# Strassen's seven products of each pair of gemms, spread farther apart, in a macaron decoder layer

## The chip, the cores and the metric

The kernel runs on one core of a Trainium2 chip. The metric is the device time of one execution in microseconds. The kernel before was timed in three runs: 2215.63 us in the median, from 2208.47 to 2218.6.

## What is computed

One decoder layer on 256 tokens of width 2048, in float32: a SwiGLU half, a mixer (attention with dilated windows beside a gated MLP), a second SwiGLU half, and a norm. The change concerns the two SwiGLU halves:

```python
D_MODEL = 2048
SEQ = 256
D_FF = 5632
...
def swiglu(x, w_gate, w_up, w_down):
    return (jax.nn.silu(x @ w_gate) * (x @ w_up)) @ w_down
...
  x = x + 1/2 * SwiGLU_1(rms(x))
  x = x + mixer
  x = x + 1/2 * SwiGLU_2(rms(x))
```

## The kernel before

**Products.** Every float32 operand is split into a high and a low part, and a product is three matmuls: high by high, high by low, low by high. The activations (256 tokens, two tiles of 128) are stationary, and a weight tile of 128 rows and 512 columns streams through. Weights are split on the way: ScalarE copies the rounded high part into `wh` (line 227), VectorE subtracts it and leaves the low part in `wl` (line 228). There are four pairs of `wh` and `wl` (`LA + 1`).

**Steps.** The weights of a gemm (512 columns) come in units of four row tiles, 1 MB in one DMA on SP's queue, into three rotating buffers `raw`. A unit makes two ordinary steps ("n" in the list `steps`) of two row tiles; one is 12 matmuls (2 row tiles, 2 token tiles, 3 products). The main loop emits the products of step i and then the splits of the step four ahead (`advance`), so that in each engine's queue the splits run four steps ahead of the matmuls. All engines work strictly through their queues in the order in which this loop writes them, so the list `steps` sets the order of everything. `at(i, fn)` puts other work (SiLU, the turning of a result through DRAM, norms) at a place in this order.

**Quads.** Two gemms on the same activations (gate and up of the same 512 columns, or two column blocks of down) share one chunk of four row tiles in which Strassen's scheme (Winograd's form) is used. The 2 x 2 blocks are: the two token tiles and the two halves of the row tiles on the side of the activations, and the two halves of the row tiles (first index) and the two gemms (second index) on the side of the weights: b11, b21, b12, b22, each of two tiles of 512 columns, 512 KB. Instead of eight block products there are seven, p1 to p7. Each is a quad step ("s") of 6 matmuls. There are 27 quads: 19 in gate/up pairs, 8 in down pairs. A gate/up pair is a cycle of 12 ordinary steps and 7 quad steps, 186 matmuls.

The order of a quad is p1, p6, p7, p5 (the list OPEN, put between the last four ordinary steps of the pair before) and p2, p4, p3 (CLOSE, put between the first four of its own), so that one ordinary step lies between two of them. Each of p1, p6, p7 and p5 adds into the same PSUM bank `x_`, and after each a copy or sum of that bank goes elsewhere before the next may add to it: after p1 ScalarE copies it into q11 (line 285), after p6 into `part` (line 289), after p7 into q21 (line 291) with a subtraction on VectorE (line 293), and after p5 VectorE adds `part` into q12 (line 295).

The weights' side of p5, p6, p7 and p4 are sums of blocks. VectorE makes three of them in a row ahead of p6's split, and one ahead of p4's (`form_of`, lines 204 to 209). The first two overwrite b11 and b12.

The blocks of a quad lie in one tile `quad`. Its room is asked for anew (`room_for`) when the last quad step, p3, of the quad before has been split; then four pieces of 512 KB follow, two behind each of the next two units.

Of the kernel before, what the change touches and what calls it, by code (L numbers as in the profile page):

```python
# [44 lines left out]
def layer(ctx: ExitStack, tc: tile.TileContext, a, out):  # L45
# [54 lines left out]
    gemms = []  # L100
    hus = []
    steps = []
    ends = []
    callbacks = []
    counter = itertools.count()
# [3 lines left out]
                          quad=quad, steps=0, begun=[False] * NT, left=[3 * nk] * NT))  # L109


    OPEN = ("p1", "p6", "p7", "p5")
    CLOSE = ("p2", "p4", "p3")

    def lay_out():
        i = 0
        while i < len(gemms):
            g = gemms[i]
            size, stage = g["group"]
            chunk = g["quad"] and g["quad"]["chunk"]  # L120
            order = [(p, q) for p in range(size) for q in range(gemms[i + p]["nk"] // 2)
                     if not g["quad"] or q // 2 != chunk]
            if stage:
                order.sort(key=lambda s: stage(*s, gemms[i + s[0]]["nk"] // 2))
            new = [("n", (gemms[i + p], q // 2, q % 2)) for p, q in order]
            if g["quad"]:
                quad = g["quad"]
                quad["gemms"] = gemms[i], gemms[i + 1]
                tail = steps[-4:]
                del steps[-4:]  # L130
                for old, form in zip(tail, OPEN):
                    steps.extend((old, ("s", (quad, form))))
                for k, form in enumerate(CLOSE):
                    new.insert(2 * k + 1, ("s", (quad, form)))
                for h in quad["gemms"]:
                    h["left"] = [3 * (h["nk"] - 4) + 6] * NT
                gemms[i + 1]["left"][1] += 18
            steps.extend(new)
            i += size
        t = -1.0  # L140
        for kind, s in steps:
            t += 1 if kind == "n" else 0.5
            ends.append(t)
            if kind == "n":
# [35 lines left out]
            SP.dma_start(raws[i][:, first:end], src[:, first + o:end + o])  # L180
            first = end

    pieces = []
    quads = []

    def room_for(quad):
        quad["raw"] = big.tile([P, 8, NC], F32, tag="C", name=f"quad{len(quads)}")
        quads.append(quad)
        pieces.extend((quad, b) for b in (0, 2, 1, 3))

    def load_piece():
        quad, b = pieces.pop(0)
        g = quad["gemms"][b // 2]
        k0 = g["rows0"] + (4 * quad["chunk"] + 2 * (b % 2)) * P
        src = g["w"][k0:k0 + 2 * P, g["c0"]:g["c0"] + NC].rearrange("(k p) c -> p k c", p=P)
        SP.dma_start(quad["raw"][:, 2 * b:2 * b + 2], src)

    def block(quad, g, j):
        return quad["raw"].rearrange("p (g q j) c -> p g j q c", g=2, q=2)[:, g, j]

    def form_of(quad, form):
        b11, b21, b12, b22 = (block(quad, g, j) for g in range(2) for j in range(2))
        if form == "p6":
            DVE.tensor_tensor(b11, b12, b11, op=OP.subtract)  # L204
            DVE.tensor_tensor(b12, b12, b22, op=OP.subtract)  # L205
            quad["sum"] = big.tile([P, 2, NC], F32, tag="k2", name="sum")
            DVE.tensor_tensor(quad["sum"], b22, b11, op=OP.subtract)  # L207
        elif form == "p4":
            DVE.tensor_tensor(b21, b21, quad["sum"], op=OP.subtract)  # L209
        return {"p1": b11, "p2": b21, "p3": b22, "p4": b21, "p5": b11, "p6": quad["sum"] if form == "p6" else None,  # L210
                "p7": b12}[form]

    place = {}

    def split(i, k=slice(0, 2)):
        kind, s = steps[i]
        if kind == "n":
            m = place[i]
            r = raws[m // 2][:, 2 * (m % 2):2 * (m % 2) + 2, :]
        else:  # L220
            r = form_of(*s)
        if i not in splits:
            wh = big.tile([P, 2, NC], F32R, tag="wh", bufs=LA + 1, name=f"wh{i}")
# [3 lines left out]
        ACT.activation(wh[:, k], r[:, k], AF.Copy)  # L227
        DVE.tensor_tensor(wl[:, k], r[:, k], wh[:, k].bitcast(F32), op=OP.subtract)  # L228
# [38 lines left out]
    def quad_products(i, quad, form):  # L267
# [7 lines left out]
        for q in range(2):  # L275
# [5 lines left out]
            for act, w in ((hi, wh), (hi, wl), (lo, wh)):  # L281
                product(g, t, act, w[:, q], q == 1 and act is lo)
        (q11, q21), (q12, x_) = first["ps"], second["ps"]
        if form == "p1":
            ACT.activation(q11, x_, AF.Copy)  # L285
            first["begun"][0] = True
        elif form == "p6":
            quad["part"] = sb.tile([P, NC], F32, tag="W", name="part")
            ACT.activation(quad["part"], x_, AF.Copy)
        elif form == "p7":  # L290
            ACT.activation(q21, x_, AF.Copy)
            first["begun"][1] = True
            DVE.tensor_tensor(quad["part"], quad["part"], x_, op=OP.subtract)
        elif form == "p5":
            DVE.tensor_tensor(q12, x_, quad["part"], op=OP.add)  # L295
            second["begun"][0] = True
        close(g, i)

# [137 lines left out]
    def ffn(wg, wu, wd, down_post, group):  # L436
        sides[0] = 0
        halves = ((0, 6), (6, 11))
        for hf, (f0, f1) in enumerate(halves):
# [8 lines left out]
            for f in range(f0, f1):  # L448
# [38 lines left out]
                quad = dict(chunk=CS, forms=lambda: xT["forms"])  # L487
                gemm(wg, f * NC, 0, KD, lhs_x, post_gate, BOTH, bank, quad)
                gemm(wu, f * NC, 0, KD, lhs_x, post_up, BOTH, bank, quad)
            for c in range(4):  # L490
                if c % 2 == 0:
                    bank = side()
                    quad = dict(chunk=0, forms=lambda st=st: st["forms"])
# [3 lines left out]
        for g in gemms:  # L497
            g.setdefault("stage", wd)

    def side():  # L500
        sides[0] += 1
# [442 lines left out]
        sgw_turn(mixer + 8 + 10 * h, h)  # L944
    at(ends[-1] - 36, load_fin)
    for after, stage in ((12, a["ffn1_w_gate"][0]), (start_of(ffn2_gate) + 1, ffn2_gate)):
        at(after, lambda: room_for(next(q for i, (k, q) in enumerate(steps) if k == "s" and not q[0].get("raw"))[0]))


    load_unit(0, (0, 1))  # L950
# [149 lines left out]
```

## Time and profile before

| | |
|---|---|
| median of three runs | 2215.63 us |
| the profiled execution | 2210.57 us |
| its span, first to last instruction | 2208.9 us |
| mean granted clock of TensorE | 0.973 |
| mean rate of the DMA engines | 213 GB/s |
| instructions | 24108 |

The profile names engines PE (matmul), PEld (weight load), DVE (VectorE), ACT (ScalarE), POOL and SP; SPq is SP's DMA queue. Tiles are named out<-in, and L227 is line 227 of the kernel. `mm` and `qd` are PSUM banks (`qd` those of quads), `raw` the units, `quad` the blocks of a quad, `sum` the sum for p6, `fpx` and `fph` the sums of activations, `hlo`, `xlo` and so on the low parts of activations. A wait is named by who waits, then who ended it.

### The profile page before, as it was taken

The page shows a single profiled execution, that of the slowest core. Times are in us where ns is not written, and L with a number is a line of the kernel's source. Part 1 is how long each engine was busy: PE and PEld are TensorE (multiplying, and loading weights), DVE is VectorE, ACT ScalarE, POOL GpSimd, SP SyncE. Part 2 cuts the span into 40 slices and gives each one's busy share as a digit, 9 for nine tenths or more (in the row PEclk, how much of TensorE's full clock was granted, in tenths as well). Part 3 has the DMA queues.
Part 4 walks back from the last instruction along what each step waited for, and adds up shares of the span by engine and source line. Part 5 has one row for each costly group of instructions (what it writes and reads, how often), then busy time and mean ns, then how long its engine had stood idle before and what let it go on. Part 6 is the DMA issues. An engine that isn't in the chain of part 4 may idle for free.

```text
span 2208.9 us, 24108 instructions
## 1 busy us (share of the span) xinstructions
PE 2063.2 (93%) x9323; PEld 1771.9 (80%) x9323; DVE 1433.9 (65%) x1463; ACT 1088.6 (49%) x1240; POOL 11.3 (1%) x19
## 2 busy tenths in 40 slices
PE   9988999998889899999999999998998899978898
PEld 8777778876678788888888888877777788867787
DVE  6666667666667567666655555666665676666675
ACT  6544455444445555454554444554444454445454
POOL 0000000000000000000000000000000000000000
PEclk9999999999999999999999999999999999999999
DMA  8655666565556876697766666865566665655563
GB/s 308 206 184 203 210 221 220 187 206 188 173 190 210 255 259 210 212 281 257 261 214 225 225 216 226 260 199 189 182 214 198 216 219 188 215 186 175 190 229 134
DMA packets 249499, 471.54 MB, mean 213 GB/s; under 512 B 12460, under 2 KB 41000, under 8 KB 249256
## 3 DMA queue, kind: packets, MB, share of 16 engines
q1 hardware_dynamic: 249064, 469.47, 63.7%
q8 instruction: 73, 1.20, 0.2%
q10 hardware_dynamic: 320, 0.53, 0.1%
q14 instruction: 42, 0.34, 0.0%
HBM read 440.30 MB, written 29.66 MB: 213 GB/s over the span
## 4 chain that ended last, share of the span: by engine, by line
PE 55%; DMA 16%; DVE 14%; ACT 7%; issue 6%; SPq 1%; ACTq 0%; DVEq 0%; POOLq 0%; POOL 0%
PE mm L237 30%; PE qd L237 24%; DMA quad<-in_ffn_w_gate_dram 5%; ACT wh L227 5%; DVE wl L228 5%; DMA raw<-in_ffn_w_up_dram 3%; DMA quad<-in_ffn_w_down_dram 3%; DVE quad L205 1%; DMA xt<-bmx 1%; DVE quad L204 1%; DVE sum L207 1%; DVE quad L209 1%; DMA raw<-in_ffn_w_down_dram 1%; DMA uroom<-bmu 1%; DVE qd L295 1%
## 5 line engine op out<-in xcount | busy, mean ns | idle before, releaser
L228 DVE TENSOR_TENSOR wl<-raw,wh 128x1024 fp32r<-128x1024 f32 (+1 forms) x665 | 800.3, 1216 | 476.0 <-ACT wh L227 474.8
L227 ACT ACTIVATE wh<-raw 128x1024 fp32r<-128x1024 f32 (+1 forms) x665 | 695.0, 1050 | 628.1 <-PE mm L237 291.2
L237 PE MATMUL qd<-wl,xhi 128*128 128x512 f32 x1026 | 400.3, 390 | 14.8 <-DVE wl L228 14.6
L237 PE MATMUL qd<-wh,xhi 128*128 128x512 f32 x1026 | 399.6, 389 | 7.5 <-ACT wh L227 7.5
L237 PE MATMUL qd<-wh,xlo 128*128 128x512 f32 x1026 | 395.9, 386 | 0.0
L237 PE MATMUL mm<-wh,xhi 128*128 128x512 f32 x928 | 352.6, 380 | 2.0 <-ACT wh L227 2.0
L237 PE MATMUL mm<-wl,xhi 128*128 128x512 f32 x928 | 350.5, 380 | 4.1 <-DVE wl L228 3.9
L237 PE MATMUL mm<-wh,xlo 128*128 128x512 f32 x928 | 351.8, 379 | 0.0
L228 DVE TENSOR_TENSOR wl<-quad,wh 128x1024 fp32r<-128x1024 f32 x162 | 197.4, 1218 | 201.4 <-ACT wh L227 112.8
L227 ACT ACTIVATE wh<-quad 128x1024 fp32r<-128x1024 f32 x162 | 169.6, 1047 | 240.5 <-DMA quad<-in_ffn_w_gate_dram 87.6
L237 PEld LDWEIGHTS qd<-wl,xhi 128*128 128x128 f32 x1026 | 199.7, 195 | 57.9 <-DVE wl L228 26.9
L237 PEld LDWEIGHTS qd<-wh,xhi 128*128 128x128 f32 x1026 | 200.4, 195 | 40.5 <-ACT wh L227 10.3
L237 PEld LDWEIGHTS qd<-wh,xlo 128*128 128x128 f32 x1026 | 198.8, 194 | 28.5
L237 PEld LDWEIGHTS mm<-wl,xhi 128*128 128x128 f32 x928 | 175.4, 189 | 31.3 <-DVE wl L228 6.7
L237 PEld LDWEIGHTS mm<-wh,xhi 128*128 128x128 f32 x928 | 175.4, 189 | 27.5 <-ACT wh L227 2.8
L237 PEld LDWEIGHTS mm<-wh,xlo 128*128 128x128 f32 x928 | 175.4, 189 | 24.9 <-DVE xlo L398 0.3
L237 PE MATMUL qd<-wh,fpx 128*128 128x512 f32 x304 | 116.8, 427 | 74.8 <-ACT qd L285 74.1
L237 PEld LDWEIGHTS qd<-wh,fpx 128*128 128x128 f32 x304 | 63.6, 209 | 91.9 <-ACT qd L285 80.9
L227 ACT ACTIVATE wh<-sum 128x1024 fp32r<-128x1024 f32 x27 | 28.5, 1056 | 136.2 <-DVE sum L207 136.2
L237 PE MATMUL qd<-wh,hhi23.0_659 128*128 128x512 f32 x172 | 65.3, 380 | 0.9 <-ACT wh L227 0.9
L237 PE MATMUL qd<-wl,hhi23.0_659 128*128 128x512 f32 x172 | 65.3, 380 | 0.8 <-DVE wl L228 0.8
L237 PE MATMUL qd<-wl,hhi522.0_10636 128*128 128x512 f32 x172 | 65.3, 380 | 0.4 <-DVE wl L228 0.4
(400 smaller groups left out, 2289.3 us busy)
## 6 DMA issues: line engine op xcount, KB each, us to landing
raw<-in_w_in_dram SPq DMA_DIRECT2D x92, 1024.0 KB, 5.4
raw<-in_ffn_w_down_dram SPq DMA_DIRECT2D x72, 1024.0 KB, 5.3
raw<-in_ffn_w_gate_dram SPq DMA_DIRECT2D x66, 1024.0 KB, 5.2
raw<-in_ffn_w_up_dram SPq DMA_DIRECT2D x66, 1024.0 KB, 5.2
quad<-in_ffn_w_gate_dram SPq DMA_DIRECT2D x38, 512.0 KB, 7.8
quad<-in_ffn_w_up_dram SPq DMA_DIRECT2D x38, 512.0 KB, 8.7
quad<-in_ffn_w_down_dram SPq DMA_DIRECT2D x32, 512.0 KB, 8.5
raw<-in_w_out_dram SPq DMA_DIRECT2D x16, 1024.0 KB, 5.1
```

Source lines behind the costliest of these rows:

```text
L204: DVE.tensor_tensor(b11, b12, b11, op=OP.subtract)
L205: DVE.tensor_tensor(b12, b12, b22, op=OP.subtract)
L207: DVE.tensor_tensor(quad["sum"], b22, b11, op=OP.subtract)
L209: DVE.tensor_tensor(b21, b21, quad["sum"], op=OP.subtract)
L227: ACT.activation(wh[:, k], r[:, k], AF.Copy)
L228: DVE.tensor_tensor(wl[:, k], r[:, k], wh[:, k].bitcast(F32), op=OP.subtract)
L237: PE.matmul(g["ps"][t], act, in_turn(w), start=not g["begun"][t], stop=g["left"][t] == 0, skip_group_check=g["quad"] is not None)
L295: DVE.tensor_tensor(q12, x_, quad["part"], op=OP.add)
```

## The change

It does five things.

- The quad steps lie farther apart: p1, two ordinary steps, p6, two, p7, two (with the border of the pairs between), p5, two, p3, one, p2, one, p4.
- The four sums on VectorE are no longer made at p6 and p4. Each stands ahead of the split of another step (`prepared`): t1 = b12 - b11 two steps ahead of p1, t3 = b12 - b22 one step ahead of p1, t2 = b22 - t1 on the step behind p1, and t4 = b21 - t2 on the step ahead of p5. t1 and t2 have places of their own, so that b11 is no longer overwritten; t4 overwrites t2.
- There is one room for the blocks of all quads of an FFN. A block of the next quad is loaded into the place of the same block of this one, as soon as the quad step that reads it has been split: b11 after p1, b12 after p7, b22 after p3, b21 after p2.
- The first quad of an FFN has all four blocks loaded at once.
- The tile `part` is now part of a tile with t1.

```diff
-    OPEN = ("p1", "p6", "p7", "p5")
-    CLOSE = ("p2", "p4", "p3")
+    OPEN = ((5, "p1"), (3, "p6"), (1, "p7"))
+    CLOSE = ((1, "p5"), (3, "p3"), (4, "p2"), (5, "p4"))
...
-                tail = steps[-4:]
-                del steps[-4:]
-                for old, form in zip(tail, OPEN):
-                    steps.extend((old, ("s", (quad, form))))
-                for k, form in enumerate(CLOSE):
-                    new.insert(2 * k + 1, ("s", (quad, form)))
+                for k, form in OPEN:
+                    steps.insert(len(steps) - k, ("s", (quad, form)))
+                for k, form in reversed(CLOSE):
+                    new.insert(k, ("s", (quad, form)))
+                quads.append(quad)
...
     def room_for(quad):
-        quad["raw"] = big.tile([P, 8, NC], F32, tag="C", name=f"quad{len(quads)}")
-        quads.append(quad)
-        pieces.extend((quad, b) for b in (0, 2, 1, 3))
-
-    def load_piece():
-        quad, b = pieces.pop(0)
-        g = quad["gemms"][b // 2]
-        k0 = g["rows0"] + (4 * quad["chunk"] + 2 * (b % 2)) * P
-        src = g["w"][k0:k0 + 2 * P, g["c0"]:g["c0"] + NC].rearrange("(k p) c -> p k c", p=P)
-        SP.dma_start(quad["raw"][:, 2 * b:2 * b + 2], src)
+        quad["room"] = (big.tile([P, 4, 2, NC], F32, tag="C", name="quads"), big.tile([P, 2, NC], F32, tag="k2", name="sum"),
+                        sb.tile([P, 3, NC], F32, tag="W", name="part"))
+        for b in (0, 2, 3, 1):
+            load_block(quad, b)
+
+    def load_block(quad, b):
+        if quad is None:
+            return
+        if "room" not in quad:
+            quad["room"] = quads[quads.index(quad) - 1]["room"]
+        g, j = quad["gemms"][b // 2], b % 2
+        k0 = g["rows0"] + 4 * quad["chunk"] * P
+        src = g["w"][k0:k0 + 4 * P, g["c0"]:g["c0"] + NC].rearrange("(q j p) c -> p j q c", p=P, j=2)
+        SP.dma_start(quad["room"][0][:, b], src[:, j])
+
+    def blocks_of(quad):
+        r = quad["room"]
+        return [r[0][:, b] for b in range(4)] + [r[1], r[2][:, 1:3], r[2][:, 0]]
+
+    def prepare(quad, what):
+        b11, b21, b12, b22, t2, t1, _ = blocks_of(quad)
+        out, x, y = {"t1": (t1, b12, b11), "t3": (b12, b12, b22), "t2": (t2, b22, t1), "t4": (t2, b21, t2)}[what]
+        DVE.tensor_tensor(out, x, y, op=OP.subtract)
...
+    FREES = {"p1": 0, "p2": 1, "p7": 2, "p3": 3}
...
     def split(i, k=slice(0, 2)):
+        for quad, what in prepared.pop(i, []):
+            prepare(quad, what)
...
-        if kind == "s" and s[1] == "p3":
-            later = [q for k, q in steps[i + 1:] if k == "s" and q[0] is not s[0]]
-            if later and later[0][0]["gemms"][0]["stage"] == s[0]["gemms"][0]["stage"]:
-                room_for(later[0][0])
+        if kind == "s" and s[1] in FREES:
+            load_block(next_of(s[0]), FREES[s[1]])
...
+    for i, (kind, s) in enumerate(steps):
+        if kind == "s" and s[1] == "p6":
+            for k, what in ((-5, "t1"), (-4, "t3"), (-2, "t2"), (5, "t4")):
+                prepared.setdefault(i + k, []).append((s[0], what))
...
                 loaded += 1
-                for _ in pieces[0:2]:
-                    load_piece()
             split(done)
```

**Three places in the order of the instructions.** The first two are at the third gate/up quad of the first FFN. VectorE before, from an ordinary split through p1's (`wl_1348<-quad`) to p6's (`wl_1390<-sum`) and p7's:

```order
L228 TENSOR_TENSOR wl_1331<-raw_1258,wh_1330 128x1024
L228 TENSOR_TENSOR wl_1348<-quad_1235,wh_1347 128x1024
L228 TENSOR_TENSOR wl_1366<-raw_1258,wh_1365 128x1024
L316 TENSOR_TENSOR hlo23.0_660<-sg40.5_1032,hhi23.0_659 128x1024
L204 TENSOR_TENSOR quad_1235<-quad_1235 128x2x512
L205 TENSOR_TENSOR quad_1235<-quad_1235 128x2x512
L207 TENSOR_TENSOR sum<-quad_1235 128x1024
L228 TENSOR_TENSOR wl_1390<-sum,wh_1389 128x1024
L228 TENSOR_TENSOR wl_1406<-raw_1292,wh_1405 128x1024
L228 TENSOR_TENSOR wl_1421<-quad_1235,wh_1420 128x1024
```

VectorE after, from t1 (`part<-quads`) through t3 (`quads<-quads`), p1's split (`wl_1317`) and t2 (`sum<-quads,part`) to p6's split (`wl_1366<-sum`):

```order
L211 TENSOR_TENSOR part<-quads 128x1024
L236 TENSOR_TENSOR wl_1288<-raw_1137,wh_1287 128x1024
L211 TENSOR_TENSOR quads<-quads 128x1024
L236 TENSOR_TENSOR wl_1301<-raw_1184,wh_1300 128x1024
L236 TENSOR_TENSOR wl_1317<-quads,wh_1316 128x1024
L211 TENSOR_TENSOR sum<-quads,part 128x1024
L236 TENSOR_TENSOR wl_1329<-raw_1184,wh_1328 128x1024
L236 TENSOR_TENSOR wl_1348<-raw_1237,wh_1347 128x1024
L236 TENSOR_TENSOR wl_1366<-sum,wh_1365 128x1024
```

The three sums that stood in a row ahead of p6's split now each have a split or two behind them, and the last stands two splits ahead of it.

ScalarE before, from p1's split (`wh_1347`) to p7's (`wh_1420`); `wh_1389<-sum` is p6's, and line 285 is the copy after p1 for which p6's products wait:

```order
L227 ACTIVATE wh_1347<-quad_1235 128x1024
L455 ACTIVATE sg56.0_1346<-qd_0_1099,rstd_456 128x512
L455 ACTIVATE sg56.0_1346<-qd_1_1100,rstd_456 128x512
L227 ACTIVATE wh_1365<-raw_1258 128x1024
L315 ACTIVATE hhi23.0_659<-sg40.5_1032 128x1024
L227 ACTIVATE wh_1389<-sum 128x1024
L227 ACTIVATE wh_1405<-raw_1292 128x1024
L285 ACTIVATE qd_0_1409<-qd_3_1412 128x512
L227 ACTIVATE wh_1420<-quad_1235 128x1024
```

ScalarE after, from p1's split (`wh_1316`) to p7's (`wh_1416`); line 292 is the same copy:

```order
L235 ACTIVATE wh_1316<-quads 128x1024
L235 ACTIVATE wh_1328<-raw_1184 128x1024
L235 ACTIVATE wh_1347<-raw_1237 128x1024
L461 ACTIVATE sg56.0_1344<-qd_0_1062,rstd_462 128x512
L461 ACTIVATE sg56.0_1344<-qd_1_1063,rstd_462 128x512
L235 ACTIVATE wh_1365<-sum 128x1024
L292 ACTIVATE qd_0_1369<-qd_3_1372 128x512
L235 ACTIVATE wh_1380<-raw_1237 128x1024
L321 ACTIVATE hhi23.0_663<-sg40.5_1033 128x1024
L235 ACTIVATE wh_1400<-raw_1297 128x1024
L235 ACTIVATE wh_1416<-quads 128x1024
```

The copy still stands behind p6's split, but now directly; there are two ordinary splits on either side of p6's in place of one.

SP's queue before, the first twelve rows of a gate/up cycle of the first FFN counted from a turning; `bmh` and `sg` are the turning of a result through DRAM:

```order
L327 DMA bmh63.5_1539<-bth63.5_1536 128x1024
L180 DMA raw_1568<-in_ffn_w_up_dram 128x4x512
L196 DMA quad_1545<-in_ffn_w_gate_dram 128x2x512
L196 DMA quad_1545<-in_ffn_w_up_dram 128x2x512
L333 DMA sg56.0_1346<-bmh63.5_1539 32x4x256 x4
L180 DMA raw_1602<-in_ffn_w_up_dram 128x4x512
L196 DMA quad_1545<-in_ffn_w_gate_dram 128x2x512
L196 DMA quad_1545<-in_ffn_w_up_dram 128x2x512
L180 DMA raw_1638<-in_ffn_w_gate_dram 128x4x512
L180 DMA raw_1693<-in_ffn_w_gate_dram 128x4x512
L180 DMA raw_1758<-in_ffn_w_gate_dram 128x4x512
L180 DMA raw_1815<-in_ffn_w_up_dram 128x4x512
```

SP's queue after, a gate/up cycle of the first FFN counted in the same way:

```order
L333 DMA bmh48.0_1235<-bth48.0_1232 128x1024
L181 DMA raw_1237<-in_ffn_w_up_dram 128x4x512
L202 DMA quads<-in_ffn_w_gate_dram 128x2x512
L339 DMA sg40.5_1033<-bmh48.0_1235 32x4x256 x4
L181 DMA raw_1297<-in_ffn_w_up_dram 128x4x512
L202 DMA quads<-in_ffn_w_gate_dram 128x2x512
L181 DMA raw_1345<-in_ffn_w_gate_dram 128x4x512
L181 DMA raw_1398<-in_ffn_w_gate_dram 128x4x512
L202 DMA quads<-in_ffn_w_up_dram 128x2x512
L181 DMA raw_1444<-in_ffn_w_gate_dram 128x4x512
L181 DMA raw_1491<-in_ffn_w_up_dram 128x4x512
L202 DMA quads<-in_ffn_w_up_dram 128x2x512
```

The four block loads that stood in two pairs between two units are now single, with one or two units between them.

More of the change, by code (lines that the diff above doesn't have):

```diff
@@ L102, in layer @@
     steps = []
+    quads = []
+    prepared = {}
     ends = []
@@ L283, in quad_products @@
         (q11, q21), (q12, x_) = first["ps"], second["ps"]
+        part = blocks_of(quad)[-1]
         if form == "p1":
@@ L287, in quad_products @@
         elif form == "p6":
-            quad["part"] = sb.tile([P, NC], F32, tag="W", name="part")
-            ACT.activation(quad["part"], x_, AF.Copy)
+            ACT.activation(part, x_, AF.Copy)
         elif form == "p7":
@@ L292, in quad_products @@
             first["begun"][1] = True
-            DVE.tensor_tensor(quad["part"], quad["part"], x_, op=OP.subtract)
+            DVE.tensor_tensor(part, part, x_, op=OP.subtract)
         elif form == "p5":
-            DVE.tensor_tensor(q12, x_, quad["part"], op=OP.add)
+            DVE.tensor_tensor(q12, x_, part, op=OP.add)
             second["begun"][0] = True
@@ L486, in ffn @@
                 bank = side()
[L487 removed]
+                quad = dict(chunk=CS, forms=lambda: xT["forms"], stage=wd)
                 gemm(wg, f * NC, 0, KD, lhs_x, post_gate, BOTH, bank, quad)
@@ L946, in layer @@
     for after, stage in ((12, a["ffn1_w_gate"][0]), (start_of(ffn2_gate) + 1, ffn2_gate)):
-        at(after, lambda: room_for(next(q for i, (k, q) in enumerate(steps) if k == "s" and not q[0].get("raw"))[0]))
+        at(after, lambda: room_for(next(q for q in quads if "room" not in q)))
+    for i, (kind, s) in enumerate(steps):
+        if kind == "s" and s[1] == "p6":
+            for k, what in ((-5, "t1"), (-4, "t3"), (-2, "t2"), (5, "t4")):
+                prepared.setdefault(i + k, []).append((s[0], what))
     load_unit(0, (0, 1))
```

23 lines of the change are left out of this document (6 added, 17 removed).

## The prediction, made before the changed kernel had run

> **What bounds the kernel now.** I read the page first (who is busy), then the waits of TensorE, then the timeline of one quad, then windows. TensorE is busy almost throughout:
>
> ```profile
> PE 2063.2 (93%) x9323; PEld 1771.9 (80%) x9323; DVE 1433.9 (65%) x1463; ACT 1088.6 (49%) x1240; POOL 11.3 (1%) x19
> ```
>
> So the time is the matmuls plus what TensorE loses. Its waits say where it loses (us in total, times, longest):
>
> ```profile
> PE qd L237 <- ACT qd L285: 91.8, 22, 8.4
> PE qd L237 <- DVE wl L228: 20.6, 33, 1.8
> PE qd L237 <- ACT wh L227: 14.2, 12, 3.5
> PE qd L237 <- DVE part L293: 3.5, 3, 1.5
> ```
>
> Two thirds is one wait, 22 times over 27 quads: p6 adds into the bank that p1 filled, and waits until ScalarE has copied it out (L285). That copy is 0.58 us long and needs only p1, so the question is what stands ahead of it. The timeline of the second gate/up cycle answers that (start, duration; in brackets the idle time before and its end):
>
> ```profile
> 163.84 0.37 SPq L180 DMA_DIRECT2D raw<-in_ffn_w_up_dram  x1
> 164.26 0.50 SPq L196 DMA_DIRECT2D quad<-in_ffn_w_gate_dram  x1
> ...
> 170.32 0.37 SPq L196 DMA_DIRECT2D quad<-in_ffn_w_up_dram  x1
> ...
> 179.60 1.06 ACT L227 ACTIVATE wh<-quad 128x1024 fp32r<-128x1024 f32 x1 [8.97 <-DMA quad<-in_ffn_w_gate_dram]
> ...
> 183.93 1.22 DVE L316 TENSOR_TENSOR hlo23.0_660<-sg40.5_1032,hhi23.0_659 128x1024 fp32r<-128x1024 f32 x1
> 185.06 1.22 DVE L204 TENSOR_TENSOR quad<-quad 128x1024 f32<-128x1024 f32 x1
> ...
> 188.79 1.06 ACT L227 ACTIVATE wh<-sum 128x1024 fp32r<-128x1024 f32 x1 [5.09 <-DVE sum L207]
> 189.76 1.04 ACT L227 ACTIVATE wh<-raw 128x1024 fp32r<-128x1024 f32 x1
> 190.70 0.58 ACT L285 ACTIVATE qd<-qd 128x512 f32<-128x512 f32 x1
> ...
> 191.34 0.79 PE L237 MATMUL qd<-wh,fpx 128*128 128x512 f32 x1 [4.63 <-ACT qd L285]
> ```
>
> The next quad's four blocks are issued in a heap with two whole units between 163.84 and 170.32. The blocks land late, so p1's split starts 9 us late and the lead of the splits over TensorE is used up. Then three sums run on VectorE back to back, ScalarE stands 5.09 us behind them with p6's split, the copy stands behind that, and TensorE stops for 4.63 us. Over the run the same two causes:
>
> ```profile
> ACT wh L227 <- DVE sum L207: 136.2, 27, 5.6
> ACT wh L227 <- DMA quad<-in_ffn_w_gate_dram: 87.6, 12, 9.8
> DVE wl L228 <- DMA quad<-in_ffn_w_up_dram: 79.3, 10, 8.8
> ```
>
> The wait on the sums occurs in all 27 quads, the stop of TensorE in 22: late loads and bunched sums together make it. There is a second loss. In these windows (length, busy time and count of each engine, granted clock, DMA share, GB/s) the matmuls after the stop run at half clock, and the burst of loads fills the DMA engines at 330 GB/s:
>
> ```profile
> 191.30:197.00 5.70, 5.67 (x13) 4.53 (x14) 4.43 (x4) 3.44 (x4) 0.00 (x0) 0.50 0.17 35
> 164.00:180.00 16.00, 15.89 (x74) 13.58 (x72) 5.67 (x5) 3.72 (x5) 0.00 (x0) 1.00 0.99 330
> 961.00:1422.00 461.00, 460.99 (x2181) 405.08 (x2182) 277.58 (x301) 224.88 (x256) 0.00 (x0) 1.00 0.74 238
> ```
>
> 13 matmuls in 5.7 us where 2.8 would do: 2.9 us on top of the stop. The last row is the mixer, which has no quads: 461 us with no stop, full clock, at 238 GB/s. The chain of waits gives there the price of a matmul that waits for nothing:
>
> ```profile
> 1147.22 274.56 PE mm L237 x1272
> ```
>
> 274.56/1272 = 0.2158 us. An ordinary step (12 matmuls) is 2.59 us, a quad step (6) 1.29 us, and a gate/up cycle (12 ordinary, 7 quad steps: 186 matmuls) 40.1 us.
>
> **The change, part by part.** No matmul, split, sum, copy or load is added or removed: each engine's instruction counts stay, and each quad still has four 512 KB loads. The sum is made against the profiled execution, 2210.57 us, of which 2208.9 are span; the median of the runs, 2215.63, is 5 us above.
>
> *Term 1, the whole gate/up cycles.* 13 of them lie in windows of one cycle each, of which the first, the last and the sum are:
>
> ```profile
> 139.00:189.00 50.00, 43.58 (x186) 36.50 (x186) 31.97 (x30) 22.66 (x26) 0.00 (x0) 0.93 0.57 190
> ...
> 2038.00:2087.00 49.00, 42.91 (x186) 36.01 (x186) 31.98 (x30) 22.45 (x26) 0.00 (x0) 0.97 0.58 193
> sum 652.00, PE 564.75 PEld 474.38 DVE 425.71 ACT 299.13 POOL 0.00; mean PE 43.44 PEld 36.49 DVE 32.75 ACT 23.01 POOL 0.00
> ```
>
> 652.0 - 13 x 186 x 0.2158 = 652.0 - 521.8 = 130.2 us lost, 10 in each cycle. I take all of it as gained, for these reasons.
>
> The sums. They now stand one by one ahead of four different splits: 1.22 us each instead of 3.7 us in a row. The third sum stands two splits ahead of p6's. With four split buffers a split starts when the step four before it is done, so three steps remain to it; in the new order the narrowest three are two quad steps and one ordinary, 1.29 + 2.59 + 1.29 = 5.2 us, against 1.05 + 1.22 for the split. 2.9 us are left for one sum and one small VectorE step. VectorE has 31.98 us of work in a cycle, now to be done in 40.1 (80%).
>
> The copies. Between p1 and p6, p6 and p7, p7 and p5 now lie two ordinary steps, 5.2 us instead of 2.6. Ahead of the copy stands one split of 1.05 us, so about 1.7 us after p1 it is done.
>
> The loads. A block of the next quad goes out when the split that used that place last is done. The shortest time is that of b22: from p3's split to the sum t3 lie three ordinary and two quad steps, 10.4 us; b12 has 20 us, the others more. The quad loads took, from issue to landing:
>
> ```profile
> DMA to landing us min/median/max: 5.8/8.7/11.2
> ```
>
> The median fits; the longest is 0.8 us late, inside the 2.9 us. Spread out, they should be nearer the shortest. Bytes per cycle are 193 GB/s x 49 us = 9.5 MB; in 40.1 us that is 236 GB/s, the rate of the mixer row, which had no stop.
>
> The SP queue. Each block load now waits there for a split, and ordinary units stand behind it: at most one step, 2.6 us late. A unit lands 5.2 us after its issue (row below) and has four ordinary and two quad steps, 13 us, until its split. No cost; if this cover goes, see the second rival.
>
> ```profile
> raw<-in_ffn_w_gate_dram SPq DMA_DIRECT2D x66, 1024.0 KB, 5.2
> ```
>
> *Term 2, the other stretches with quads:* first and last cycles of a half, and the down gemms.
>
> ```profile
> 75.00:139.00 64.00, 56.29 (x248) 47.14 (x246) 44.45 (x46) 28.63 (x33) 0.00 (x0) 0.97 0.60 198
> 288.00:500.00 212.00, 204.85 (x936) 177.44 (x936) 143.90 (x136) 105.54 (x111) 0.00 (x0) 0.99 0.61 208
> 652.00:756.00 104.00, 98.13 (x442) 84.36 (x443) 70.95 (x69) 54.35 (x68) 2.80 (x5) 0.98 0.65 211
> 1474.00:1523.00 49.00, 44.68 (x203) 37.55 (x201) 32.69 (x35) 26.19 (x29) 0.00 (x0) 1.00 0.62 211
> 1723.00:1936.00 213.00, 205.19 (x936) 177.94 (x936) 144.57 (x137) 105.43 (x111) 0.00 (x0) 0.98 0.60 208
> 2087.00:2200.00 113.00, 108.17 (x485) 93.37 (x486) 78.36 (x85) 57.58 (x70) 0.55 (x1) 0.97 0.49 172
> sum 755.00, PE 717.31 PEld 617.80 DVE 514.93 ACT 377.73 POOL 3.35; mean PE 119.55 PEld 102.97 DVE 85.82 ACT 62.95 POOL 0.56
> ```
>
> 3250 matmuls x 0.2158 = 701.4; 53.6 us lost. Not all is the quads': the units of the down matrix also come late there:
>
> ```profile
> ACT wh L227 <- DMA raw<-in_ffn_w_down_dram: 32.0, 11, 5.4
> ```
>
> Most of these 32 us are covered by the lead; bounds are 0 and 32 for what stays, and I keep 9, nearer to 0 because only the waits over about 3 us can reach TensorE. Gain 45. As a check, the two views of the loss agree: TensorE's quad waits above add up to 130.1, and half clock costs (1 - 0.973) x 2208.9 = 59.6 with the mean granted clock of the run; together 190, against 130 + 54 = 184 by windows.
>
> ```profile
> core 0: 2208.9 us, clock 0.973
> ```
>
> On that half clock the Trainium skill's page TensorE: Matmul & The Clock Gate (Part 1: The HAM clock gate) says that about 3.4 us of sustained work bring full clock back. By that a stop would cost 1.7 us on top, 46 over 27 quads, and the gain would be 14 us smaller; this trace has 5.7 us at half clock after a stop, so I go by the row.
>
> *Term 3, what gets worse.* At the start of each FFN the first quad's four blocks now go out at once, 2 MB ahead of the next unit instead of 1 MB: 3.2 us at 330 GB/s, twice. In the second FFN a load on the chain stands behind them:
>
> ```profile
> 1453.80 9.24 DMA xt<-bmx
> ```
>
> There I charge the 3.2 in full, in the first, where no such load is near, 1. Bounds 0 and 6.4; taken 4.
>
> Sum: 2210.6 - 130.2 - 45 + 4 = 2039.4 for an execution like the profiled one, up to 2044 for one like the median. I say 2041.
>
> **Rivals.**
> *Stops that stay, smaller.* VectorE at 80% and the 10.4 us for b22 are the tight places; a block that lands late now holds VectorE's whole queue at t3. If half of the 27 quads keep a stop of 3 us with its 2.9 us at half clock: 13.5 x 5.9 = 80 us, 2121; with 2 us in each quad 54, 2095. For it: 11.2 us landings exist. Against: they come from the burst.
> *The SP queue starves the units (slower).* A block load waits in the queue for a split, the split waits for TensorE, and the unit behind it starts late. It decides from the point where the loss per quad passes 184/27 = 6.8 us, a stop of 4 us with its half clock; for that a unit must land 13 + 2.9 + 4 = 20 us after its issue time in my table. Say 8.3 us in each: 2041 + 27 x 8.3 = 2265. Against: 5.2 us is the median landing.
> *The heap only moves.* If the blocks, interleaved with the units, arrive as late as before, the copies wait as before: 2210.
>
> **How the numbers follow.** Forecast 0.80 (own spread 2022 to 2080: with the whole 53.6 of term 2 gained and no new cost it is 2027, less a little scatter; with the 32 us of late units kept in full 2064, and with 0.6 us of wait left in each of 27 quads 2080). Smaller stops 0.14 (2085 to 2130), queue starved 0.03, moved heap 0.03. Range 2022 to 2088. About 0.5% (11 us) is what a measurement of this kernel tells from no change: faster 0.94, same 0.03, slower 0.03.
>
> **What would show it.** Right: the wait of p6 on the copy is gone from TensorE's waits; the wait of wh<-sum on its sum is near 0 and no quad block is waited for by ScalarE or VectorE longer than 2 us; a gate/up cycle takes 40 to 41 us at about 235 GB/s; granted clock 0.99 or more. Wrong: a new wait of VectorE's first or second sum on a block (the loads), of TensorE on wl (VectorE too full), or of wh<-raw on units (the queue). The prediction falls if cycles stay above 43 us.

## The result, and the profile after

The changed kernel takes 2026.5 us in the median of four runs (2025.94 to 2032.22) against 2213.53 us before (2208.47 to 2218.6): a ratio of 0.916, with a 95% interval from 0.913 to 0.919. The forecast was 2041, with a range from 2022 to 2088. In the profiled execution the span went from 2208.9 to 2024.2 us, 184.7 us less.

First, of the changed kernel (called "after" from here on), the page's line of busy engines, and the span with TensorE's mean clock. TensorE has the same 9323 matmuls and is now busy for 99% of a shorter span:

```profile
PE 2002.4 (99%) x9323; PEld 1750.0 (86%) x9323; DVE 1437.0 (71%) x1463; ACT 1105.7 (55%) x1240; POOL 11.3 (1%) x19
```

```profile
core 0: 2024.2 us, clock 0.997
```

TensorE's waits after (us in total, times, longest). The wait for the copy, 91.8 us in 22 times before, is gone, and no other has taken its place:

```profile
PE qd L243 <- ACT wh L235: 5.2, 2, 4.7
PE mm L243 <- ACT wh L235: 1.9, 1, 1.9
PE qd L243 <- DVE wl L236: 1.8, 1, 1.8
PE mm L243 <- DVE wl L236: 1.7, 2, 1.0
PE qd L243 <- DVE qd L301: 1.4, 1, 1.4
```

The chain of waits after (start, length). Where the chain before was broken in every cycle, it now runs through almost the whole of each half as one piece of matmuls:

```profile
108.30 515.66 PE qd L243 x2388
...
663.64 9.66 DMA xt<-bmx
...
1395.46 615.14 PE qd L243 x2850
```

515.66/2388 = 0.2159 us and 615.14/2850 = 0.2158 us: the price of a matmul that waits for nothing. A window over the first of the two (length, busy time and count of PE, PEld, DVE, ACT and POOL, granted clock, DMA share, GB/s) shows full clock and the rate of the loads:

```profile
108.30:623.90 515.60, 515.60 (x2389) 451.48 (x2390) 397.92 (x373) 289.65 (x302) 0.00 (x0) 1.00 0.72 230
```

Last, the tile of the blocks: what its instructions on ScalarE and VectorE waited for. Before:

```profile
  DMA quad<-in_ffn_w_up_dram: 105.5, 13
  DMA quad<-in_ffn_w_gate_dram: 87.6, 12
...
  DMA quad<-in_ffn_w_down_dram: 40.6, 5
```

and after, with its loads' time from issue to landing:

```profile
  PE qd L243: 141.6, 93
  ACT wh L235: 49.3, 58
  PE mm L243: 3.4, 3
  DVE wl L236: 1.5, 1
...
DMA to landing us min/median/max: 3.5/3.8/11.4
```

Before, 233.7 us in 30 waits were for a block's load. After, no wait for one is listed (the first four lines are the whole list); the wait of the splits is now for TensorE (141.6 us), which means that they are ahead of it. The loads land in 3.8 us in the median instead of 8.7.

### The profile page after: what moved, and what is told of

The parts are those of the page before. It is cut to its first block, busy times and chain, and to the rows that moved or that the text cites. A ratio compares the mean times of both kernels' runs of the same rounds, so it can differ in the third digit from the quotient of the medians.

```text
span 2024.2 us, 24110 instructions
## 1 busy us (share of the span) xinstructions
PE 2002.4 (99%) x9323; PEld 1750.0 (86%) x9323; DVE 1437.0 (71%) x1463; ACT 1105.7 (55%) x1240; POOL 11.3 (1%) x19
## 4 chain that ended last, share of the span: by engine, by line
PE 93%; DMA 2%; DVE 2%; ACT 1%; issue 1%; SPq 0%; POOLq 0%; POOL 0%; ACTq 0%; DVEq 0%
PE qd L243 57%; PE mm L243 35%; DMA xt<-bmx 1%; DMA more<-in_ffn_w_gate_dram 1%; DVE wl L236 1%; ACT xt L430 0%; ACT wh L235 0%; DMA raw<-in_ffn_w_down_dram 0%; DMA raw<-in_ffn_w_gate_dram 0%; ACT xhi L321 0%; DVE btx L349 0%; PE sp L646 0%; DMA bmx<-btx 0%; SPq L339 0%; PE pv L812 0%
## 5 line engine op out<-in xcount | busy, mean ns | idle before, releaser
L243 PE MATMUL qd<-wh,xhi 128*128 128x512 f32 x1026 | 388.9, 379 | 0.0
L243 PE MATMUL qd<-wl,xhi 128*128 128x512 f32 x1026 | 388.9, 379 | 0.0
L243 PE MATMUL qd<-wh,xlo 128*128 128x512 f32 x1026 | 388.9, 379 | 0.0
L243 PEld LDWEIGHTS qd<-wh,xhi 128*128 128x128 f32 x1026 | 193.9, 189 | 27.7
L235 ACT ACTIVATE wh<-quads 128x1024 fp32r<-128x1024 f32 x108 | 114.0, 1055 | 146.5 <-PE qd L243 141.6
L236 DVE TENSOR_TENSOR wl<-quads,wh 128x1024 fp32r<-128x1024 f32 x108 | 131.4, 1217 | 50.1 <-ACT wh L235 49.3
L243 PE MATMUL qd<-wh,fpx 128*128 128x512 f32 x304 | 102.9, 379 | 1.4 <-DVE qd L301 1.4
L236 DVE TENSOR_TENSOR wl<-sum,wh 128x1024 fp32r<-128x1024 f32 x54 | 66.1, 1225 | 37.0 <-ACT wh L235 35.3
L235 ACT ACTIVATE wh<-sum 128x1024 fp32r<-128x1024 f32 x54 | 57.1, 1057 | 29.2 <-PE qd L243 18.1
```

The lines of the kernel that those rows point to most:

```text
L243: PE.matmul(g["ps"][t], act, in_turn(w), start=not g["begun"][t], stop=g["left"][t] == 0, skip_group_check=g["quad"] is not None)
```

## The experiments

The change moves four things at once: the loads go out singly into the place of the last quad's, the sums stand ahead, the quad steps lie farther apart, and, in the same function as the first, a load is cut in another way. Before, a piece was two *neighbouring* row tiles of a gemm, while a block is row tiles 0 and 2 or 1 and 3, so that each block consisted of half of two pieces. `load_block` loads one whole block. The prediction did not price that. The first experiments had two theories: theory 1, that the loss came from the loads that landed late, theory 2, that it came from the sums in a row and the short distances.

All medians and ratios to the kernel before, from runs of the same job:

| experiment | us | ratio (95%) |
|---|---|---|
| old order, sums in a row, whole blocks loaded in place | 2095.48 | 0.949 (0.946 to 0.952) |
| old order, sums ahead, whole blocks in a heap | 2074.71 | 0.938 (0.936 to 0.940) |
| old order, sums in a row, whole blocks in a heap | 2074.83 | 0.938 (0.936 to 0.941) |
| old order, sums ahead, row pairs in a heap | 2176.15 | 0.983 (0.980 to 0.986) |
| new order, sums in a row, in place | 2040.99 | 0.923 (0.921 to 0.926) |
| old order, sums ahead, in place | 2028.68 | 0.918 (0.916 to 0.919) |
| after, four block loads together | 2062.64 | 0.932 (0.930 to 0.933) |
| after, b22 two quad steps later | 2034.53 | 0.918 (0.917 to 0.920) |
| after, lead of three steps | 2068.47 | 0.934 (0.933 to 0.936) |
| before, lead of three steps | 2248.07 | 1.015 (1.013 to 1.016) |
| after, once more | 2027.92 | 0.919 (0.916 to 0.921) |
| after, starts reordered | 2019.54 | 0.915 (0.913 to 0.917) |

### The loads alone

Old order and sums in a row, so that b11 and b21 are freed where their sums are made:

```diff
-    OPEN = ((5, "p1"), (3, "p6"), (1, "p7"))
-    CLOSE = ((1, "p5"), (3, "p3"), (4, "p2"), (5, "p4"))
+    OPEN = ((3, "p1"), (2, "p6"), (1, "p7"), (0, "p5"))
+    CLOSE = ((1, "p2"), (2, "p4"), (3, "p3"))
...
-    FREES = {"p1": 0, "p2": 1, "p7": 2, "p3": 3}
+    FREES = {"p6": 0, "p4": 1, "p7": 2, "p3": 3}
...
-            for k, what in ((-5, "t1"), (-4, "t3"), (-2, "t2"), (5, "t4")):
+            for k, what in ((0, "t1"), (0, "t3"), (0, "t2"), (8, "t4")):
```

> The old order of the quad steps and the three sums in a row ahead of p6's split, but each block loaded into the place of the last quad's as soon as it is free. Theory 1 (late blocks are the trigger; the sums and the copy only pass the delay on): no split waits for a block over 2 us, the wait of p6's split on its sum stays at about 5 us in all 27 quads (136 us), but the lead of the splits absorbs nearly all of it: by hand 0.5 to 1 us of TensorE's time per quad is left, 2035 to 2055 us. Theory 2 (the sums in a row and the near copies stop TensorE by themselves): the wait on L285's copy stays in most quads at 3 to 5 us with half clock behind it, 2100 to 2150 us.

It took 2095.48 us: 114 of the 187 us, between the ranges of the two theories and close to the second's. TensorE's wait on the copy is still there 18 times, and, new, ScalarE waits for the units:

```profile
PE qd L243 <- ACT qd L292: 38.8, 18, 6.0
...
ACT wh L235 <- DMA raw<-in_ffn_w_up_dram: 85.6, 21, 5.6
```

and in the list of DMA issues the up units take 8.3 us to land, against 5.8 after:

```profile
raw<-in_ffn_w_up_dram SPq DMA_DIRECT2D x66, 1024.0 KB, 8.3
```

That is the prediction's rival of the starved queue, in small: a block load waits in SP's queue, and the units behind it are late.

### The sums ahead, loads in a heap

The old order again, the sums ahead, and the four loads asked for at p3's split, two behind each of the next two units, as before:

```diff
-        if kind == "s" and s[1] in FREES:
-            load_block(next_of(s[0]), FREES[s[1]])
+        if kind == "s" and s[1] == "p3" and next_of(s[0]) is not None:
+            pieces.extend((next_of(s[0]), b) for b in (0, 2, 3, 1))
...
-            for k, what in ((-5, "t1"), (-4, "t3"), (-2, "t2"), (5, "t4")):
+            for k, what in ((-4, "t1"), (-3, "t3"), (-1, "t2"), (3, "t4")):
...
+                for _ in pieces[0:2]:
+                    load_block(*pieces.pop(0))
```

> The old order and the old loads (four pieces behind two units, after p3), but the sums one by one ahead and in places of their own. Theory 1: the blocks land as late as before, VectorE now stands at the first or second sum for 8 us or so, two steps earlier in its queue than before, and TensorE still stops in every gate/up cycle: 2150 to 2220 us. Theory 2: the stop loses the 3.7 us of the sums and with it most of its half clock: 2060 to 2120 us.

2074.71 us. Theory 1, as it was put, is refuted: the heap lands as late as before (8.6 us in the median), and yet nearly three quarters of the gain are there. Theory 2's number was met, but the next two runs show that it was not for theory 2's reason: this kernel also loads whole blocks.

```profile
DVE quads L212 <- DMA quads<-in_ffn_w_up_dram: 55.9, 15, 4.9
DVE part L212 <- DMA quads<-in_ffn_w_up_dram: 47.6, 15, 5.4
...
PE qd L244 <- DVE wl L237: 23.2, 20, 3.1
```

VectorE, whose sums now come earlier than the blocks, waits for them some 3.5 us at a time, and only a part reaches TensorE.

### The cut of the loads by itself

Two kernels part the two. In the first the sums go back into a row ahead of p6 and p4; so it differs from the kernel before in the cut of the loads, their order (b11, b12, b22, b21), and the one room for all quads with places of their own for t1 and t2:

```diff
-            for k, what in ((-4, "t1"), (-3, "t3"), (-1, "t2"), (3, "t4")):
+            for k, what in ((0, "t1"), (0, "t3"), (0, "t2"), (8, "t4")):
```

> The old order, the three sums in a row at p6, and the four loads behind two units as before; but each load is one whole block, in the order b11, b12, b22, b21, and p1's sums no longer overwrite b11. It is the run with the sums ahead only, less the sums ahead. Account 1 (in that run the sums being ahead did the work): 2180 to 2215 us, near before. Account 2 (whole blocks did it, since p1 needs one load instead of three): p1's split waits less than 3 us for its block and the sums take the wait: 2100 to 2150 us.

In the second the sums stay ahead, and the pieces are pairs of neighbouring row tiles again, in the order of before:

```diff
-        pieces.extend((quad, b) for b in (0, 2, 3, 1))
+        pieces.extend((quad, b) for b in (0, 2, 1, 3))
...
-        src = g["w"][k0:k0 + 4 * P, g["c0"]:g["c0"] + NC].rearrange("(q j p) c -> p j q c", p=P, j=2)
-        SP.dma_start(quad["room"][0][:, b], src[:, j])
+        src = g["w"][k0:k0 + 2 * P, g["c0"]:g["c0"] + NC].rearrange("(j p) c -> p j c", p=P)
+        SP.dma_start(quad["room"][0][:, b // 2 * 2:b // 2 * 2 + 2, q], src)
```

> The old order and the sums one by one ahead, with the pieces of before: each load is two neighbouring row tiles of a gemm, so that b11 and b12 need pieces 1 to 4 all. Account 1: as the run with the sums ahead only, 2070 to 2090 us. Account 2: t1 waits for the last piece, 3 to 4 us longer than in that run, and TensorE stops longer: 2110 to 2160 us.

They took 2074.83 and 2176.15 us. Whole blocks, with those places, give 139 us of the gain, more than either account had said. Beside them the sums ahead add nothing (2074.71 against 2074.83); with the old pieces they give 38. With sums ahead in both, the cut and the order of the loads are worth 101 us (2176.15 against 2074.71).

In the first kernel the blocks land as late as in the kernel before, and not one of its instructions waits for a block. Its tile of blocks has:

```profile
  PE qd L244: 35.3, 23
  ACT wh L236: 31.8, 25
  PE mm L244: 1.5, 1
...
DMA to landing us min/median/max: 5.7/8.4/11.4
```

Its timeline, beside the prediction's fence of the kernel before, tells why. It is taken one gate/up cycle earlier than that fence; the next cycle has the same waits, 5.09 us for the sum and 0.6 us on TensorE.

```profile
116.62 0.50 SPq L203 DMA_DIRECT2D quads<-in_ffn_w_gate_dram  x1
...
124.44 1.06 ACT L236 ACTIVATE wh<-quads 128x1024 fp32r<-128x1024 f32 x1 [1.53 <-PE qd L244]
...
134.12 1.06 ACT L236 ACTIVATE wh<-sum 128x1024 fp32r<-128x1024 f32 x1 [5.09 <-DVE sum L212]
...
136.66 0.48 PE L244 MATMUL qd<-wh,fpx 128*128 128x512 f32 x1 [0.61 <-ACT qd L293]
```

p1's split (124.44) needs the first load only, issued 7.8 us earlier, and had been held up by TensorE, not by a load. In the kernel before, half of b11 is in the third piece, behind another unit and the transfers of a turned block:

```profile
165.37 2.31 SPq L333 DMA_DIRECT2D sg40.5_1032<-bmh48.0_1229  x4
167.73 0.43 SPq L180 DMA_DIRECT2D raw<-in_ffn_w_up_dram  x1
169.07 0.39 SPq L196 DMA_DIRECT2D quad<-in_ffn_w_gate_dram  x1
```

That piece went out at 169.07, and ScalarE, which was ready for p1's split at 170.6 (179.60 less its 8.97 us of idle time), stood until it landed. With whole blocks ScalarE waits the same 5.09 us behind the three sums, but the lead is whole when it comes to them, and TensorE stops for 0.61 us instead of 4.63. The cycle is 41.02 us (from 136.66 to the next such piece of the chain at 177.68) where it was 49 to 53:

```profile
136.66 31.37 PE qd L244 x144
177.68 31.37 PE qd L244 x144
```

In the second kernel the sum t1 needs all four pieces, and it stands at the head of VectorE's queue:

```profile
126.95 1.22 DVE L212 TENSOR_TENSOR part<-quads 128x1024 f32<-128x1024 f32 x1 [12.46 <-DMA quads<-in_ffn_w_up_dram]
```

```profile
DVE part L212 <- DMA quads<-in_ffn_w_up_dram: 157.4, 15, 12.5
...
PE qd L244 <- DVE wl L237: 94.6, 22, 7.4
```

### Distance and sums in the new loads

The new order with the sums in a row at p6, and the places freed where the sums are made:

```diff
-    FREES = {"p1": 0, "p2": 1, "p7": 2, "p3": 3}
+    FREES = {"p6": 0, "p4": 1, "p7": 2, "p3": 3}
...
-            for k, what in ((-5, "t1"), (-4, "t3"), (-2, "t2"), (5, "t4")):
+            for k, what in ((0, "t1"), (0, "t3"), (0, "t2"), (13, "t4")):
```

> The changed kernel, but t1, t3 and t2 in a row ahead of p6's split and t4 at p4; b11 is then loaded after p6 and b21 after p4. Theory 1: with the blocks on time and two ordinary steps ahead of p6 the lead covers 3.7 us of sums: 2026 to 2035 us, the split of p6 waits about 4 us for its sum and TensorE does not. Theory 2: a stop of 1 to 3 us per quad stays, with half clock 2060 to 2110 us.

The old order with the sums ahead, else as after:

```diff
-    OPEN = ((5, "p1"), (3, "p6"), (1, "p7"))
-    CLOSE = ((1, "p5"), (3, "p3"), (4, "p2"), (5, "p4"))
+    OPEN = ((3, "p1"), (2, "p6"), (1, "p7"), (0, "p5"))
+    CLOSE = ((1, "p2"), (2, "p4"), (3, "p3"))
...
-            for k, what in ((-5, "t1"), (-4, "t3"), (-2, "t2"), (5, "t4")):
+            for k, what in ((-4, "t1"), (-3, "t3"), (-1, "t2"), (3, "t4")):
```

> The changed kernel's loads and its sums one by one, but the old order with one ordinary step between two quad steps. Theory 1: one ordinary step, 2.6 us, is more than the 1.7 us in which the copy is done; no stop comes back, 2026 to 2040 us. Theory 2 (the distance is what matters): p6 waits for the copy again, 0.5 to 1.5 us per quad, 2040 to 2070 us.

2040.99 and 2028.68 us. Without the distance the kernel is as fast as after (0.918 against 0.916 and 0.919 in its two measurements): the distance, which gave the change its name, is worth nothing that these runs can tell once the sums stand ahead and the blocks are loaded in place. With the sums in a row it is worth 54 us (2095.48 to 2040.99), and with the distance the sums ahead are worth 10 to 15 (0.923 to 0.919 and 0.916), hardly more than the intervals. One does the other's work. The loads in place are the opposite: in the old order with whole blocks, loads in place without the sums ahead lose some 20 us (2074.83 to 2095.48), the sums ahead without them bring nothing (2074.71), and both together bring 46 (2028.68).

In the kernel of the new order with the sums in a row ScalarE still stands behind the sums in every quad; the lead takes nearly all of it:

```profile
ACT wh L235 <- DVE sum L211: 182.9, 54, 6.2
...
PE qd L243 <- ACT wh L235: 10.8, 5, 6.0
```

In the kernel of the old order ScalarE waits for units (46.4 us, 16 times), and next to nothing of it reaches TensorE, whose products in the quads wait for `wh` once, 3.7 us.

```profile
ACT wh L235 <- DMA raw<-in_ffn_w_up_dram: 46.4, 16, 5.6
```

### Loads together, and one load late

After, with all four loads at p2's split:

```diff
-        if kind == "s" and s[1] in FREES:
-            load_block(next_of(s[0]), FREES[s[1]])
+        if kind == "s" and s[1] == "p2":
+            for b in (0, 2, 3, 1):
+                load_block(next_of(s[0]), b)
```

> The changed kernel's order and sums, but the four blocks of the next quad in one heap when the last of them is free, after p2. Between p2's split and t1 lie one ordinary and one quad step, 3.9 us, and 2 MB take 6.4 us at 330 GB/s behind what is in flight, so VectorE stands at t1 or t3 for 4 to 8 us. Additive account (lateness of blocks plus work in a row, less the lead of the splits): a stop of 2 to 5 us in each of 27 quads, with half clock behind it, 2110 to 2230 us. If loads matter little once the sums are ahead: 2030 to 2060 us.

and after, with b22 two quad steps later:

```diff
-    FREES = {"p1": 0, "p2": 1, "p7": 2, "p3": 3}
+    FREES = {"p1": 0, "p2": 1, "p7": 2, "p4": 3}
```

> The changed kernel, with b22 loaded after p4's split instead of p3's, 7.8 us later, so that one ordinary step (2.6 us) is left until t3. A block lands 3.8 us after its issue in the median of the changed kernel, so t3 is some 1 to 3 us late. Additive account: the lead (2.9 us at its narrowest) covers it, VectorE waits for b22 in most quads and TensorE does not: 2026 to 2040 us. If the lead is already used up: a stop of 1 to 3 us per quad, 2050 to 2110 us.

2062.64 and 2034.53 us. The heap costs 29 to 34 us here (by the ratios, 0.932 against 0.919 and 0.916), far less than the 84 us and more of the additive account, by which the lateness of the blocks, less the lead, stops TensorE for 2 to 5 us in each quad. VectorE's waits in the first kernel, what is left of them on TensorE, and VectorE's waits in the second:

```profile
DVE part L211 <- DMA quads<-in_ffn_w_up_dram: 63.5, 15, 5.7
...
PE qd L244 <- DVE wl L236: 26.1, 18, 4.0
```

```profile
DVE quads L211 <- DMA quads<-in_ffn_w_up_dram: 38.6, 14, 5.2
...
PE qd L243 <- DVE wl L236: 7.3, 7, 2.0
```

4.2 us of wait at a time become 1.5 us on TensorE, and 2.8 become 1.0 in half of the cases.

### The lead

The lead of the splits over the matmuls is what takes these waits. With three steps instead of four:

```diff
-LA = 3
+LA = 2
```

> The changed kernel with three pairs of split buffers instead of four: the splits run three steps ahead. By the prediction's table at the narrowest place (one ordinary and one quad step, 3.9 us, against 2.3 us for a split) 1.6 us are left for a sum of 1.2 us and other VectorE work. Additive account: small stops of 0.5 to 1 us in some quads, 2030 to 2060 us. If the fourth buffer carries the gain: above 2090 us.

> The kernel before with three pairs of split buffers instead of four. Additive account: the lateness that the lead covered, one step of 1.3 to 2.6 us, comes onto TensorE in every gate/up quad, and in the down quads, where the sums had been covered, a stop appears: 27 x 2 to 2.6 us and some more half clock, 2260 to 2300 us. If the stops do not depend on the lead: within 10 us of before.

After took 2068.47 us, 34 to 40 more by the ratios; before 2248.07, 33 more and less than expected. In the first kernel the cycles hold even so, for some 1600 matmuls in one piece at 0.216 and 0.217 us; it loses at the starts and at the turning of results:

```profile
111.08 340.82 PE qd L243 x1577
...
1463.47 357.88 PE qd L243 x1649
```

In the kernel before, the waits for blocks shrink with the shorter lead (ScalarE's for gate blocks from 87.6 us to 26.6), so that the stops do not simply grow by the step that was taken away:

```profile
ACT wh L227 <- DMA quad<-in_ffn_w_gate_dram: 26.6, 10, 4.5
```

### What is left: the starts

The largest break left in after is the mixer's start: the mixer's constants are issued in one row ahead of the transfer that the first product of the mixer needs (issued at 662.04 us, on the chain until 673.3):

```profile
659.76 1.67 SPq L546 DMA_DIRECT2D ln<-in_sg_ln_g_dram  x1
...
662.04 2.34 SPq L339 DMA_DIRECT2D xt<-bmx  x4
```

So the constants were put behind it, and the four loads of the first quad of the first FFN four steps later; two turnings of a result in the mixer (`sgw_turn`) move along:

```diff
-    at(mixer - 9, mixer_consts)
+    at(mixer + 6, mixer_consts)
...
-        sgw_turn(mixer + 8 + 10 * h, h)
+        sgw_turn(mixer + 11 + 9 * h, h)
...
-    for after, stage in ((12, a["ffn1_w_gate"][0]), (start_of(ffn2_gate) + 1, ffn2_gate)):
+    for after, stage in ((16, a["ffn1_w_gate"][0]), (start_of(ffn2_gate) + 1, ffn2_gate)):
```

> The changed kernel, with two of its remaining losses addressed: the mixer's constants (seven loads, 2.3 MB in three of them) are asked for 15 steps later, so that they no longer stand ahead of the turned column block of x for which TensorE waits at the mixer's start (about 7.7 us of stop and 1.9 us at half clock in the changed kernel), and the first quad's 2 MB go out four steps later. If these bursts cause the waits: 8 to 12 us less than the changed kernel in the same job, 2014 to 2019 us. If the wait is the length of the turning itself: within 3 us of it.

Beside it ran the changed kernel itself once more:

> The changed kernel unaltered, as the control for the run beside it: 2025 to 2032 us.

2019.54 us (2016.38 to 2021.36) against 2027.92 (2023.06 to 2034.2): 8.4 us less, and the ranges do not meet. The parts of this edit were not run apart. In the profiles the first unbroken piece of matmuls starts 1.9 us earlier than in after (106.37 against 108.30 us), and the mixer's piece of 600 matmuls 11.1 us earlier (678.42 against 689.48), so most of it is the mixer's start. Of TensorE's waits in the quads' products for `wh`, 5.2 us in after, this is left:

```profile
PE qd L243 <- ACT wh L235: 0.5, 1, 0.5
```

This is the fastest version that was run.

## Why the prediction was right, and where not

*The bound and the unit price: right.* TensorE was the bound, the loss was its stops and the half clock behind them, and the loss by windows, 184 us, is what the span lost: 184.7. On the half clock the row was the better guide: by the prediction's estimate from the Trainium skill's page TensorE: Matmul & The Clock Gate (Part 1: The HAM clock gate) the gain would have been 14 us smaller, 2055 for the forecast.

*Term 1, 130.2 us in whole gate/up cycles: right in full.* Both long pieces of the chain run at 0.216 us a matmul with the cycles inside, 40.1 us each for 186, at 230 GB/s over the first of them, down gemms among it, against the 236 that the prediction gave for the cycles alone.

*Term 2: mis-sized.* It took 45 of 53.6 us, and kept 9 for late units. The down gemms lie in the same two unbroken pieces, so nearly all of the 53.6 came. The units of the down matrix hardly came late any more: ScalarE's waits for them fell from 32.0 us in 11 waits to 5.0 in 2:

```profile
ACT wh L235 <- DMA raw<-in_ffn_w_down_dram: 5.0, 2, 3.8
```

*Term 3: wrong in sign, and small.* It charged 4 us. TensorE's waits at the start of the first FFN grew from 0.8 to 2.9 us, and at that of the second shrank from 3.9 to 0.8: about 1 us less in all. 130.2 + 53.6 + 1 is 184.8, against 184.7 measured. That the two meet so closely is partly luck, for some changes are in no term: TensorE's waits at the mixer's start grew from 5.3 to 7.0 us.

*The cause of the late split of p1: the step that failed.* "The blocks land late" took the heap and its 8.7 us of landing for the cause. A heap that lands in 8.4 us, in the old places of the order and with the sums still in a row, loses 0.9 us in most cycles instead of 10. What was late was the *third* piece, because b11 was spread over the first and the third. The row of 169.07 us was left out of the prediction's fence (it stood under the "..."), and the new line of `load_block` that changes the cut was in the diff and was not priced. That the total came right all the same is partly luck: the changed kernel cuts the loads anew and does away with the heap as well.

*"Late loads and bunched sums together make it": right for the sums, wrong for the loads.* The sums in a row are nearly harmless when b11 comes early: with whole blocks TensorE stops for 0.61 us. The loads of the old cut do harm without the row too: with the sums ahead t1 waits for all four pieces, and only 38 us come back.

*The copies two steps away, priced inside term 1, have no measurable value of their own* with the sums ahead (0.918 against 0.916 and 0.919).

*The rivals.* Smaller stops did not stay, nor did the heap only move. The starved queue did not occur in after, where SP's block loads wait 325.9 us in all for the splits (95 times, 3.4 us on average and up to 9.0, where the prediction let what stands behind them be 2.6 us late at most), but with the old order: 85.6 us of ScalarE's waits with sums in a row, 46.4 with sums ahead. In after and with the sums ahead the lead covers it, as "no cost" said; with the old order and the sums in a row the loads in place are 0.011 of the time, some 20 us, slower than the heap of whole blocks (0.949 against 0.938). That the late units make this difference is likely but was not run by itself.

*What stays open.* The places of their own for t1 and t2 were not run apart from the whole blocks; in the pair that differs in the cut and order of the pieces alone it is worth 101 us, in the other, with those places, 139. The traces give the places no part in it: neither in the kernel before nor with whole blocks in a heap does a block load wait in SP's queue for a split or a sum, only for other transfers (39.7 and 41.6 us in all, 42 times each). And what the last heap costs (44 to 49 us by the ratios, from whole blocks in a heap to after) was located only in part: by the chain the 13 whole gate/up cycles lose 17 us, 0.9 to 1.0 in ten of them and 2.5 to 3.0 in three, while the down gemms run unbroken (169.93 us for 786 matmuls, 193.25 for 894). The rest lies in the first and last cycles of the halves and at the starts, and was not taken apart.

## What to carry to other kernels

Ask for each load which consumer needs it first, and cut and order the loads so that this consumer needs one of them: a block spread over two pieces is as late as the second, whatever the median landing says. Remedies for one chain can replace each other (here sums ahead and steps apart) or pay only together (here sums ahead and loads in place), so price a part only beside the others. What a wait on a helper engine costs is read from the busy engine behind the lead: with a lead of four steps between a seventh and a third of VectorE's waits for blocks, those of the down gemms counted in, arrived as TensorE's waits for `wl` (23.2 of 132.3 us with the sums ahead and the heap, 26.1 of 81.8 with the loads together, 7.3 of 49.0 with b22 late).

## What the runs showed of the hardware that was not expected

Short stops in a row can be followed by the half clock too. In the kernel before, two stops of 0.93 and 0.78 us within 1.3 us are followed, a us later, by matmuls 0.43 us apart instead of 0.22 (the granted clock from 282.3 to 285.7 us is 0.51):

```profile
280.02 0.48 PE L237 MATMUL qd<-wh,hhi23.0_659 128*128 128x512 f32 x1 [0.93 <-ACT wh L227]
281.28 0.48 PE L237 MATMUL qd<-wl,hhi23.0_659 128*128 128x512 f32 x1 [0.78 <-DVE wl L228]
...
284.39 0.63 PE L237 MATMUL qd<-wh,xhi 128*128 128x512 f32 x1
284.82 0.63 PE L237 MATMUL qd<-wl,xhi 128*128 128x512 f32 x1
```

The single stop of 0.61 us in the kernel with whole blocks in a heap left the clock at 1.00 in its window:

```profile
120.00:160.00 40.00, 39.39 (x183) 34.10 (x182) 31.46 (x30) 22.27 (x25) 0.00 (x0) 1.00 0.65 227
```

These are one place each; where the limit lies between them, no run here shows.
